# Moving the loads of the last merged-head tiles and the first MLP product at the seam between attention and the MLP of an encoder layer

## The chip, the core and the metric

The kernel runs on one core of one Trainium2 chip. The metric is the device time in microseconds. Shares of the span and times of single instructions come from one execution taken with the hardware profiler.

## What is computed

One encoder layer over 2048 tokens of width 1024: a mixer (eight stick-breaking heads, eight heads of banded softmax attention) and a squared-ReLU MLP, each behind an RMSNorm with shift, scale and gate from a conditioning vector. All in float32.

```python
h = rmsnorm(x, g_norm1[l]) * (1.0 + sc1) + sh1
proj = h @ w_in[l]
...
mixed = jnp.concatenate([o_sb.reshape(B, S, D_SB), o_ca.reshape(B, S, D_CA)], axis=-1)
x = x + gt1 * (mixed @ w_o[l])
h = rmsnorm(x, g_norm2[l]) * (1.0 + sc2) + sh2
x = x + gt2 * (jnp.square(jax.nn.relu(h @ w1[l])) @ w2[l])
```

## The kernel before

Tokens are worked on in four blocks of 512 (TB), the width in eight tiles of 128 (KT = 8); everything is kept transposed, 128 rows of width by 512 tokens. Each float32 operand is split into a high part (a cast on ScalarE, ACT) and a low part (a subtraction on VectorE, DVE), and a product of two is three matmuls on TensorE (PE): a projection of one output tile is 8 tiles x 3 = 24 matmuls of 512 columns. The compiler keeps the order in which the program emits instructions on each engine; DMA loads and stores are issued by SyncE (SP), in that order too.

The attention stage writes the merged heads of token block g, split, into scr_m[g, k] in DRAM (line 803), k = 0 to 7; the stores of the last block (0) are issued by GpSimd (POOL), the very last of them, k = 7, by ACT. Then the output projection of block 1, begun as filler work between the attention's own, is finished, eight rows n (matmuls po, weights ow, residual rows txr from the input), and that of block 0 follows as the steps of class Mixed (line 1974): matmuls pso, which read the eight merged tiles opm_k and weights ow or wo. Mixed.fetch (line 1984) asks for opm_k from scr_m[0, k]. Mixed runs eight steps, n = 5, 6, 7, 0 to 4, with residual rows cxr; a row's result goes to DRAM as scr_x[g, n].

Beside these products the MLP's left side is made for token blocks 3 and 2: right_blocks(1, k) (line 1503) for four values of k. For each k, load asks for four tiles of the normed residual (named ty for k = 0, cy for the rest, from scr_x); DVE multiplies them with the norm row, ACT shifts them, and casts on ACT and subtractions on DVE make seven operands h_1 to h_7 of them, as a fast matrix product of the Strassen and Winograd kind needs. some(k, n) calls piece n of block k: some(0, 0) is the load of ty, some(0, 1) its scaling.

The MLP's steps follow in one list with Mixed's: steps[0] to steps[7] are Mixed, steps[8] (KT) on are class First (line 1587), each one of the seven half-size products in the order OUTER = (1, 5, 6, 3, 7, 2, 4). First.prepare splits a weight tile (opr for the first two, opw for the rest), First.run (line 1630) emits 12 matmuls. Products 1 and 2 share a bank ps, 5 and 3 a second, 6, 7 and 4 a third, ps_s, which starts as a copy of product 1:

```python
if i == 1:
    d["ps", 6] = bank(f"{nm}_s", seeded)
    act.copy(d["ps", 6], ps)
if i in (5, 6):
    d["p", i] = kept(f"p{nm}")
    act.copy(d["p", i], ps)
```

So ACT copies bank 1 to ps_s before product 6, and the banks of products 5 and 6 out to cp before products 3 and 7 add to them.

The order around the change is written out by hand in lines 2104 to 2116: row() emits the rest of one po row (with at most two finished rows' stores held back), and the fetches and pieces stand between the rows. Then the loop of line 2130 runs the steps: for each it prepares coming operands as far as eight buffers reach, runs the jobs listed for the step, and emits its matmuls.

One more thing sets the order at run time. Each DMA that SP or ACT issues adds to one of eight semaphores, named DMAHW0 to DMAHW7, given out in turn as the program is built, and waits until the DMA that had the semaphore last has landed. A waiting issue holds up all that stands behind it on SP.

## Time and profile before

| what | before |
|---|---|
| median of 3 runs | 2511.53 us (2509.88 to 2512.42) |
| span of the profiled execution | 2511.4 us |
| instructions | 39512 |
| PE busy | 2497.0 us (99%) |
| DVE busy | 2027.0 us (81%) |
| ACT busy | 1526.4 us (61%) |
| POOL busy | 787.5 us (31%) |
| DMA | 704.71 MB, mean 281 GB/s |

Of the profiled execution no time is given beside its span; the span stands for it. A row of a timeline gives the start and the length in microseconds from the span's start, the engine (SPq is SP's queue), the source line, the operation, output and inputs by the program's names without their numbers, the shape, and how many alike are merged; in brackets stand the idle time of the engine ahead of the row and what ended it. All operations are recorded by a helper in line 42, so lines tell nothing and names do. PEld is PE's load of weights, which runs beside the matmuls.

### The profile page before, as it was taken

The page shows a single profiled execution, that of the slowest core. Times are in us where ns is not written, and L with a number is a line of the kernel's source. Part 1 is how long each engine was busy: PE and PEld are TensorE (multiplying, and loading weights), DVE is VectorE, ACT ScalarE, POOL GpSimd, SP SyncE. Part 2 cuts the span into 40 slices and gives each one's busy share as a digit, 9 for nine tenths or more (in the row PEclk, how much of TensorE's full clock was granted, in tenths as well). Part 3 has the DMA queues.
Part 4 walks back from the last instruction along what each step waited for, and adds up shares of the span by engine and source line. Part 5 has one row for each costly group of instructions (what it writes and reads, how often), then busy time and mean ns, then how long its engine had stood idle before and what let it go on. Part 6 is the DMA issues. An engine that isn't in the chain of part 4 may idle for free.

```text
span 2511.4 us, 39512 instructions
## 1 busy us (share of the span) xinstructions
PE 2497.0 (99%) x12364; PEld 2093.5 (83%) x12364; DVE 2027.0 (81%) x3571; ACT 1526.4 (61%) x2928; POOL 787.5 (31%) x1174
## 2 busy tenths in 40 slices
PE   9999999999999999999999999999999999999999
PEld 7888888888888888888888888888888888888887
DVE  7656776897789888999868777779877759799998
ACT  6334434778876687666855555567555546577765
POOL 4330144777776677776710000000000000010100
PEclk9999999999999999999999999999999999999999
DMA  9879978789888788866786878996998996888982
GB/s 368 316 301 360 357 274 289 231 263 309 268 263 264 233 252 264 274 193 216 215 321 251 298 284 309 324 354 197 325 326 271 313 364 261 320 250 280 307 277 83
DMA packets 295970, 704.71 MB, mean 281 GB/s; under 512 B 32080, under 2 KB 88400, under 8 KB 284112
## 3 DMA queue, kind: packets, MB, share of 16 engines
q1 hardware_dynamic: 287552, 684.35, 78.8%
q0 software_dynamic: 6768, 13.11, 2.9%
q10 hardware_dynamic: 1440, 4.72, 0.5%
q8 instruction: 98, 1.61, 0.3%
q14 instruction: 112, 0.92, 0.1%
HBM read 473.99 MB, written 228.07 MB: 280 GB/s over the span
## 4 chain that ended last, share of the span: by engine, by line
PE 88%; DVE 4%; DMA 4%; ACT 2%; issue 1%; SPq 0%; POOL 0%; DVEq 0%; ACTq 0%; POOLq 0%
PE ps L42 23%; PE ps_s L42 15%; PE pt L42 11%; PE acc L42 8%; PE wt L42 7%; PE pf L42 6%; PE z L42 5%; PE po L42 4%; PE pq L42 3%; PE cz L42 2%; PE pso L42 1%; PE ct L42 1%; DMA opm<-scr_m 1%; DMA hw<-in_w_dram 1%; PE px L42 1%
## 5 line engine op out<-in xcount | busy, mean ns | idle before, releaser
L42 ACT CAST wth<-wt 128x512 fp32r<-128x512 f32 (+3 forms) x544 | 257.5, 484 | 173.7 <-PE wt L42 160.9
L42 PE MATMUL ps<-h,opw 128*128 128x512 f32 x1512 | 358.6, 389 | 0.0
L42 POOL TENSOR_TENSOR b<-p 128x512 f32<-128x512 f32 (+1 forms) x320 | 292.0, 913 | 154.1 <-DVE p L42 95.6
L42 DVE TENSOR_TENSOR wtl<-wt,wth 128x512 fp32r<-128x512 f32 (+3 forms) x544 | 291.4, 547 | 60.3 <-ACT wth L42 55.8
L42 PEld LDWEIGHTS ps<-h,opw 128*128 128x128 f32 x1512 | 283.6, 188 | 58.9
L42 PE MATMUL pt<-w,ht 128*128 128x512 f32 x1248 | 288.0, 391 | 0.0
L42 PE MATMUL ps_s<-h,opw 128*128 128x512 f32 x1152 | 277.6, 390 | 1.0 <-DVE cp L42 0.6
L42 PEld LDWEIGHTS pt<-w,ht 128*128 128x128 f32 x1248 | 232.9, 188 | 47.6
L42 DVE TENSOR_TENSOR_SCAN p<-z,p,zero 128x512 f32<-128x512 f32 x192 | 245.3, 1279 | 18.6 <-ACT z L42 14.5
L42 PEld LDWEIGHTS ps_s<-h,opw 128*128 128x128 f32 x1152 | 215.7, 188 | 47.4 <-DVE cp L42 1.5
L42 ACT CAST opr<-r 128x512 fp32r<-128x512 f32 x280 | 174.3, 623 | 118.1 <-PE ps L42 66.4
L42 PE MATMUL acc<-wth,v 128*128 128x512 f32 (+3 forms) x544 | 221.3, 410 | 0.0
L42 PE MATMUL ps<-opr,ol 128*128 128x512 f32 x960 | 220.3, 389 | 0.0
L42 PEld LDWEIGHTS ps<-opr,ol 128*128 128x128 f32 x960 | 180.1, 188 | 37.8 <-DVE opr L42 0.4
L42 ACT ACTIVATE z<-z 128x512 f32<-128x512 f32 (+1 forms) x320 | 166.7, 521 | 52.7 <-PE z L42 48.2
L42 DVE TENSOR_TENSOR opr<-r,opr 128x512 fp32r<-128x512 f32 x280 | 185.5, 683 | 13.7 <-ACT opr L42 12.5
L42 PE MATMUL acc<-wtl,v 128*128 128x512 f32 (+3 forms) x544 | 185.6, 347 | 0.0
L42 PE MATMUL z<-k,q 128*128 128x512 f32 (+3 forms) x640 | 182.8, 367 | 0.6 <-DVE p L42 0.6
L42 POOL DMA_DIRECT2D scr_x<-txu x12 | 10.4, 866 | 546.0 <-ACT txu L42 544.1
L42 PE MATMUL ps<-oph,opv 128*128 128x512 f32 x768 | 175.4, 390 | 0.3 <-DVE txo L42 0.2
L42 PE MATMUL wt<-ident,b 128*128 128x128 f32 x1088 | 170.7, 272 | 0.4 <-DVE p L42 0.4
L42 PEld LDWEIGHTS ps<-oph,opv 128*128 128x128 f32 x768 | 144.0, 188 | 31.3 <-DVE txo L42 0.6
(238 smaller groups left out, 5059.9 us busy)
## 6 DMA issues: line engine op xcount, KB each, us to landing
r<-scr_hid SPq DMA_DIRECT2D x80, 512.0 KB, 7.2
q<-scr_q SPq DMA_DIRECT2D x128, 256.0 KB, 5.1
w<-in_w_dram SPq DMA_DIRECT2D x64, 512.0 KB, 5.7
k<-scr_k SPq DMA_DIRECT2D x240, 128.0 KB, 4.6
v<-scr_v SPq DMA_DIRECT2D x120, 256.0 KB, 4.6
wa<-in_w_ada_dram SPq DMA_DIRECT2D x48, 512.0 KB, 6.3
ow<-scr_wo SPq DMA_DIRECT2D x24, 1024.0 KB, 6.6
l<-scr_t SPq DMA_DIRECT2D x20, 1024.0 KB, 7.9
```

The costliest lines, as they stand in the source:

```text
L42: return lambda *x, **y: self.tc.keep_in_program_order(f(*x, **y))
```

## The change

Two edits. In the hand-written order the four later opm tiles move forward: opm_4 and opm_5 are asked for after the first row instead of after the second row and the load of ty, and opm_6 and opm_7 after the second row, ahead of ty, instead of after the third. In the loop, steps[KT], the first MLP product, emits its matmuls and the copy to ps_s ahead of the preparing and the jobs of its turn instead of behind them.

```diff
         steps[0].fetch(0, KT // 2)
         row()
-        row()
-        some(0, 0)
         steps[0].fetch(KT // 2, KT - 2)
         row()
+        steps[0].fetch(KT - 2, KT)
+        some(0, 0)
+        row()
         some(0, 1)
-        steps[0].fetch(KT - 2, KT)
         row()
         some(0, 2)
         some(1, 0)
...
         for n, s in enumerate(steps):
+            if n == KT:
+                s.run()
             while nxt is not None and ready - used + nxt.tiles <= 8 and nxt.ready():
                 nxt.prepare()
...
-            s.run()
+            if n != KT:
+                s.run()
             used += s.frees
```

The instructions stay the same; PE and DVE keep their order. On SP the DMA issues after the load of ow_6 stood so before (each row a DMA, with the semaphores that it waits for; the first number behind a name is its row or tile k, the two after ty its place, the last a running number):

```order
L42 DMA txr_5_16974<-in_xs_dram 128x512 [waits DMAHW6_49,Pool_49]
L42 DMA ow_7_17002<-scr_wo_237 128x2048 [waits DMAHW7_49,PE_49]
L42 DMA txr_6_17004<-in_xs_dram 128x512 [waits DMAHW0_49]
L42 DMA ty_0_11_17008<-scr_x_0_216 128x512 [waits DMAHW1_49]
L42 DMA ty_0_12_17010<-scr_x_0_208 128x512 [waits DMAHW2_49]
L42 DMA ty_0_21_17012<-scr_x_4_220 128x512 [waits DMAHW3_49]
L42 DMA ty_0_22_17014<-scr_x_4_212 128x512 [waits DMAHW4_49]
L42 DMA opm_4_17016<-scr_m_4_164 128x1024 [waits DMAHW5_49,DMASW0_49]
L42 DMA opm_5_17018<-scr_m_5_165 128x1024 [waits DMAHW6_49,DMASW1_49]
```

And so they stand in the changed kernel:

```order
L42 DMA txr_5_16974<-in_xs_dram 128x512 [waits DMAHW6_49,Pool_49]
L42 DMA opm_4_16978<-scr_m_4_164 128x1024 [waits DMAHW7_49,DMASW0_49]
L42 DMA opm_5_16980<-scr_m_5_165 128x1024 [waits DMAHW0_49,DMASW1_49]
L42 DMA ow_7_17006<-scr_wo_237 128x2048 [waits DMAHW1_49,PE_49]
L42 DMA txr_6_17008<-in_xs_dram 128x512 [waits DMAHW2_49]
L42 DMA opm_6_17012<-scr_m_6_166 128x1024 [waits DMAHW3_49,DMASW2_49]
L42 DMA opm_7_17014<-scr_m_7_167 128x1024 [waits DMAHW4_49]
L42 DMA ty_0_11_17016<-scr_x_0_216 128x512 [waits DMAHW5_49]
L42 DMA ty_0_12_17018<-scr_x_0_208 128x512 [waits DMAHW6_49]
L42 DMA ty_0_21_17020<-scr_x_4_220 128x512 [waits DMAHW7_49]
L42 DMA ty_0_22_17022<-scr_x_4_212 128x512 [waits DMAHW0_49]
```

opm_4 and opm_5 now stand ahead of ow_7, opm_6 and opm_7 ahead of ty, and the wait for DMAHW0, whose last user is ACT's store to scr_m[0, 7], has passed from txr_6 to opm_5. On ACT, at the first product of the MLP, the order before was this (opw_0_6 is the weight operand of product 6 for the first pair of weight rows, ps_0_1 its bank 1, ts a sum of weights, w a weight tile):

```order
L42 CAST opr<-ts_0_1_5_17492 128x512
L42 CAST opw_0_6_17528<-ts_0_1_6_17496 128x512
L42 CAST opw_0_3_17531<-ts_0_1_3_17498 128x512
L42 CAST opw_0_7_17534<-w_1_0_17445 128x512
L42 CAST opw_0_2_17537<-w_1_0_17445 128x512
L42 CAST opw_0_4_17540<-w_1_0_17445 128x512
L42 COPY ps_0_1_s<-ps_0_1_17543 128x512
```

And it is now:

```order
L42 CAST opr<-ts_0_1_5_17492 128x512
L42 COPY ps_0_1_s<-ps_0_1_17528 128x512
L42 CAST opw_0_6_17543<-ts_0_1_6_17496 128x512
L42 CAST opw_0_3_17546<-ts_0_1_3_17498 128x512
L42 CAST opw_0_7_17549<-w_1_0_17445 128x512
L42 CAST opw_0_2_17552<-w_1_0_17445 128x512
L42 CAST opw_0_4_17555<-w_1_0_17445 128x512
```

The copy to ps_s has moved ahead of five casts of weights; nothing else on ACT has.

## The prediction

> **What bounds the kernel now.** The page comes first: its span, and the share of the engine that runs the products.

> ```profile
> span 2511.4 us, 39512 instructions
> PE 2497.0 (99%) x12364; PEld 2093.5 (83%) x12364; DVE 2027.0 (81%) x3571; ACT 1526.4 (61%) x2928; POOL 787.5 (31%) x1174
> ```

> TensorE (PE) is busy for 2497.0 of 2511.4 us, so only something that makes PE stand still, or lets it stop standing still, can move the time, and all its gaps together are 14.4 us. The span lies 0.1 us under the median of the three runs shown (2511.53; 2509.88 to 2512.42), so what the sum below adds to the span I add to the median. About 0.2%, 5.0 us, is what a measurement of this kernel can tell from no change. The change touches one place, the seam between the attention stage and the MLP, so the next view is PE's timeline there; a bracket holds the idle time ahead of a row and what ended it.

> ```profile
> 1267.34 22.00 PE L42 MATMUL po<-fx,ow 128*128 128x512 f32 x96
> 1289.18 4.26 PE L42 MATMUL pso<-opm,ow 128*128 128x512 f32 x18
> 1295.02 0.96 PE L42 MATMUL pso<-opm,ow 128*128 128x512 f32 x3 [1.57 <-DMA opm<-scr_m]
> 1296.27 11.86 PE L42 MATMUL pso<-opm,ow 128*128 128x512 f32 x51 [0.29 <-DMA opm<-scr_m]
> 1307.96 27.36 PE L42 MATMUL pso<-opm,wo 128*128 128x512 f32 x120
> 1335.16 5.60 PE L42 MATMUL ps<-h,opr 128*128 128x512 f32 x24
> 1341.17 3.06 PE L42 MATMUL ps_s<-h,opw 128*128 128x512 f32 x12 [0.41 <-ACT ps_s L42]
> ...
> 1344.23 2.72 PE ps L42 x12
> 1346.95 2.98 PE ps_s L42 x12
> ```

> The reader should see four things. A product of 24 matmuls takes 5.44 us: 27.36 us for 120 matmuls is 0.227 to 0.228 each. The 96 matmuls from 1267.34 are rows 4 to 7 of the old projection; the last of them, the one that needs ow_7, begins 72 matmuls in, at 1267.34 + 72 x 0.2275 = 1283.7. In the first row of the merged projection PE waits twice for an opm: 21 matmuls from 1289.18 should end at 1293.97 and the 22nd begins at 1296.27, so 2.3 us are lost. At 1341.17 PE waits 0.41 us for ps_s, and that group takes 3.06 instead of 2.72 us (the last two rows are from the chain of waits: start, length, what), so about 0.75 us are lost; the group at 1346.95 takes 0.26 us more than 2.72. These 3.3 us are all that the change can win here.

> What feeds the seam is the SP queue, in order: each row below is a set of DMA issues. The last two rows are the waits of SP's own queue (total, times, longest) and the chain.

> ```profile
> 1259.45 1.80 SPq L42 DMA_DIRECT2D opm<-scr_m  x4
> 1266.54 0.32 SPq L42 DMA_DIRECT2D ow<-scr_wo  x1
> 1266.96 0.38 SPq L42 DMA_DIRECT2D txr<-in_xs_dram  x1
> 1273.05 0.32 SPq L42 DMA_DIRECT2D ow<-scr_wo  x1
> 1282.28 0.33 SPq L42 DMA_DIRECT2D txr<-in_xs_dram  x1
> 1282.67 1.85 SPq L42 DMA_DIRECT2D ty<-scr_x  x4
> 1284.61 0.85 SPq L42 DMA_DIRECT2D opm<-scr_m  x2
> 1287.06 1.22 SPq L42 DMA_DIRECT2D opm<-scr_m  x2
> ...
> SPq L42 <- DMA scr_m<-os: 8.9, 1, 8.9
> ...
> 1274.59 7.68 DMA scr_m<-os
> ```

> SP issues ow_7 at 1273.05 and then nothing until 1282.28: for 8.9 us its next instruction, the load of txr_6, waits for the store of the last head pair (scr_m<-os), issued by ACT at 1274.59, which takes 7.68 us to land. That load reads nothing of the store. It waits because DMAs take eight semaphores in turn, and the one that falls to it (DMAHW0) was last given to that store. I call this the gate: whichever DMA of SP meets that semaphore stands behind the store, and all of SP behind it.

> Last, the consumers of ty, VectorE (DVE) with ScalarE (ACT), which make the MLP's operands block by block:

> ```profile
> 1286.26 0.69 DVE L42 TENSOR_TENSOR ty<-ty,r 128x512 f32<-128x512 f32 x1 [6.95 <-DMA ty<-scr_x]
> 1287.45 2.18 DVE L42 TENSOR_TENSOR ty<-ty,r 128x512 f32<-128x512 f32 x3 [0.49 <-DMA ty<-scr_x]
> 1334.19 0.68 DVE L42 TENSOR_TENSOR opr<-w,opr 128x512 fp32r<-128x512 f32 x1
> ...
> 1286.26:1298.48 12.22, 10.36 (x45) 7.85 (x44) 10.77 (x18) 7.15 (x11) 0.00 (x0) 1.00 1.02 375
> 1298.48:1310.20 11.72, 11.72 (x53) 9.72 (x52) 10.53 (x18) 6.98 (x11) 0.00 (x0) 1.00 1.04 402
> 1310.20:1321.87 11.67, 11.67 (x53) 9.65 (x52) 10.54 (x19) 6.97 (x11) 0.00 (x0) 1.00 1.04 414
> 1321.87:1333.53 11.66, 11.66 (x53) 9.67 (x52) 10.53 (x18) 7.50 (x12) 0.00 (x0) 1.00 0.77 275
> ```

> DVE waited 6.95 us for the first ty and starts at 1286.26; its fourth ty multiply ends at 1287.45 + 2.18 = 1289.63. From there four blocks follow, 12.2, 11.7, 11.7 and 11.7 us (the columns after the length are the busy times of PE, PEld, DVE, ACT): DVE works 10.5 us of each 11.7 and spends the rest handing tiles to and fro with ACT. Two rows of PE take only 10.9 us, so this chain, and not PE, sets when the first MLP operand is there: 1334.19 + 0.68 = 1334.9, against PE's arrival at 1335.16. PE's stall of 2.3 us hides nearly all that DVE is behind.

> **Part 1, the order of SP's issues.** Nothing is added or taken away; four opm, ow_7, txr_6 and four ty change places. As the rows of the program in the section on the change show, the second opm to be asked for (opm_5) now carries the wait for DMAHW0, and ow_7, txr_6, opm_6, opm_7 and the four ty all stand behind it. Before, ow_7 was ahead of the gate. So the step sooner is worth one tile: opm_4 goes out right behind txr_5, near 1267.4, and the rest of the list leaves when the gate opens.

> When does it open? The store is issued at 1274.59 as before, since ACT, DVE and POOL ahead of it are untouched. How long it takes to land without ow_7 in flight beside it (1 MB less; opm_4, 0.5 MB, in its place) the trace doesn't show. The bounds come from the landing times of all such stores (least, median, most), one load that finds the queues quiet (KB, us to landing) and a stretch in which DMA never rests (its last two columns are the DMA share and GB/s):

> ```profile
> DMA to landing us min/median/max: 2.6/3.7/8.9
> ...
> w<-in_w_dram SPq DMA_DIRECT2D x1, 512.0 KB, 3.7
> ...
> 1287.00:1314.00 27.00, 25.14 (x110) 20.10 (x109) 23.76 (x38) 17.20 (x27) 0.00 (x0) 1.00 1.03 396
> ```

> Over the kernel the stores of an os take 2.6 to 8.9 us, 3.7 in the median, and this one took 7.68. I take 3.7 and add 0.6 for the last 256 KB or so of opm_4 that may be ahead of it at the rate of the third row, 396 GB/s: 4.3, so the gate opens at 1278.9, with 1277.2 and 1282.3 as the ends. [...]

> Behind the gate the first 512 KB (opm_5) should land after 3.7 us, as the second row does, a 512 KB load that finds the queues quiet; what follows lands at 396 GB/s. ow_7 (1.05 MB, 2.65 us): 1278.95 + 3.7 + 2.65 = 1285.3. Up to the fourth ty it is ow_7 1024 KB, txr_6 256, opm_6 and opm_7 1024, ty 1024, together 3.41 MB or 8.6 us: 1278.95 + 3.7 + 8.6 = 1291.25. Multiplied by 0.69 us later, 1291.94, where before it was 1289.63: **the DVE chain starts its first block 2.3 us later** (0.6 at the early end, 5.7 at the late one). The loads of cy, cxr and wo come after; the bytes are the same in both orders, DMA is full here anyway (the row above), and their readers on DVE come 2.3 us later too, so I cost them at nothing. If that cover failed, a cy late by 1 us would add that 1 us to the chain.

> On PE, ow_7 lands at 1285.3 against 1283.7, a new wait of 1.6 us (0 and 5.0 at the ends), and the old wait of 2.3 us is gone, since opm_7 lands near 1288.6 and PE comes to it after 1294. PE reaches the first MLP product 0.7 us sooner, at 1334.5. The operand is there at 1334.9 + 2.3 = 1337.2. So the first product begins 2.0 us later than at 1335.16: what was won on PE is lost in front of DVE.

> **Part 2, the first product emitted ahead of the later casts.** The rows are of ACT, DVE and SP, in that order.

> ```profile
> 1340.55 0.57 ACT L42 COPY ps_s<-ps 128x512 f32<-128x512 f32 x1
> 1345.73 0.63 ACT L42 CAST opw<-ts 128x512 fp32r<-128x512 f32 x1 [1.50 <-DVE ts L42]
> 1346.26 0.58 ACT L42 COPY cp<-ps_s 128x512 f32<-128x512 f32 x1
> ...
> 1338.70 0.75 DVE L42 SCALAR_TENSOR_TENSOR cxr<-pso,mod,cxr 128x512 f32<-128x512 f32 x1
> 1345.01 0.69 DVE L42 TENSOR_TENSOR ts<-w 128x512 f32<-128x512 f32 x1 [2.56 <-DMA w<-in_w_dram]
> ...
> 1329.86 9.93 SPq L42 DMA_DIRECT2D scr_x<-cxr  x3
> 1339.88 0.88 SPq L42 DMA_DIRECT2D w<-in_w_dram  x2
> ```

> On ACT the copy of ps_s comes ahead of five casts of opw; nothing else moves, since PE's and DVE's order is the same. The copy now runs when the first product ends, instead of after five casts, which should take the 0.75 us away at 1341.17. The casts wait behind it, but DVE takes up the first of them only after the cxr row (1338.70), so this costs nothing; were that cover gone, it would be the copy's 0.57 us. What is late next is the group at 1346.95: it writes the bank that ACT must first copy out to cp.

> The copy to cp at 1346.26 stands behind the cast at 1345.73, which waits for DVE's ts (1345.01), which waits 2.56 us for w, which SP issues at 1339.88, right behind the last of three stores of cxr, which waits for DVE's cxr row at 1338.70, part of the same chain. Nothing of this moves forward, so the 0.75 us won at one group is waited out two groups later. I cost part 2 at nothing: 0.75 us gained at most if cp comes sooner.

> **The sum.** At the group of 1346.95 PE is held to the DVE chain: +2.3 us, and after it the order is as before and PE is the bound, so the shift stays. 2511.4 + 2.3 = 2513.7 for the span, 2513.8 beside the median: 0.09%, within what can be told from no change.

> **The rivals.** *All of it is won:* the chain from ty makes up what it loses, and PE alone sets the pace. Then the 2.3 and 0.75 us go and about 2508.5 comes out, 0.12% less. [...] For it: PE's waits at 1295.02 and 1296.27 are real, and opm_4 does leave 17 us sooner. Against it: three blocks in a row of 11.7 us with DVE at 10.5, which leave nothing to catch up with, and three of the four opm stay behind the gate. *Slower:* the store lands as late as it did, 7.68 us after its issue, because what held it was not ow_7. Then the gate opens at 1282.3, PE waits 5.0 us for ow_7 and DVE starts 5.7 us later: 2517.2, +0.23%. It decides from a store of 7.0 us on, where the chain's shift passes 5.0 us. For it: this store took 7.68 us, and 8.9 us have occurred; against it: 0.5 MB less is in the queues. *Nothing to be seen:* the gate opens at 1277.2 and the shift is some tenths, 2511.5 to 2512.

> **How the numbers follow.** The forecast (2513.8) has 0.60, all won 0.12, slower 0.15, nothing 0.13. Faster by over 0.2% would need 5.0 us where at most 3.3 are idle: 0.02 for what I don't see. Slower by over 0.2% is that rival's 0.15, a shade less since its price is close to the bound: 0.14. The remainder, 0.84, is within 0.2%. The range runs from 2510.5, the nothing case less 1 us of the runs' own spread, to the slow rival's 2517.2 and a little; it leaves out the all-won case.

> **What would show it.** In the changed kernel's profile: SP issues one opm near 1267.4 and is then idle until the store lands; ow_7 is issued behind that, at 1279 rather than 1273.05; PE has a wait ahead of the last po row of 0 to 5 us, and none for opm; the first ty multiply on DVE begins near 1289 to 1290, not 1286.26; PE waits ahead of the first ps for DVE's opr; the wait for ps_s at the second group is gone and a longer one for cp stands two groups later. I am wrong if ow_7 still leaves near 1273, if DVE's blocks shrink below 11.7 us, or if the group that stood at 1346.95 comes earlier than it did.

## The result, and the profile after

The changed kernel takes 2514.87 us in the median (2513.35 to 2516.27), the kernel before 2511.73 us in the same series (2509.26 to 2514.12). The ratio is 1.0013, with a 95% interval of 1.0007 to 1.0019: slower by 3.1 us, 1.8 to 4.8. The profiled execution has a span of 2513.6 us, 2.2 us over that of before, and PE's busy time is nearly the same, so the loss is again time in which PE stands still, or runs slowly.

```profile
span 2513.6 us, 39511 instructions
PE 2497.8 (99%) x12364; PEld 2095.1 (83%) x12364; DVE 2028.4 (81%) x3571; ACT 1527.2 (61%) x2928; POOL 788.5 (31%) x1174
```

PE's timeline at the seam, in the changed kernel:

```profile
1266.38 16.56 PE L42 MATMUL po<-fx,ow 128*128 128x512 f32 x72
1283.90 5.72 PE L42 MATMUL po<-fx,ow 128*128 128x512 f32 x24 [0.96 <-DMA ow<-scr_wo]
1289.46 16.48 PE L42 MATMUL pso<-opm,ow 128*128 128x512 f32 x72
1305.78 27.36 PE L42 MATMUL pso<-opm,wo 128*128 128x512 f32 x120
1335.47 0.76 PE L42 MATMUL ps<-h,opr 128*128 128x512 f32 x2 [2.33 <-ACT opr L42]
1336.94 8.03 PE L42 MATMUL ps<-h,opr 128*128 128x512 f32 x22 [0.71 <-DVE opr L42]
...
1350.24 2.88 PE L42 MATMUL ps_s<-h,opw 128*128 128x512 f32 x12
```

This execution arrives at the seam 0.96 us ahead of that of before (its first row here is the one that stood at 1267.34). That is chance, as no instruction ahead of it changed place: near the program's start the granted clock was 0.50 for 3.4 us (from 15.09), against 6.8 us (from 14.83) in the execution of before, and the lead is there from then on. Against that start, ow_7 costs PE a new wait of 0.96 us, and the two waits for opm are gone: 72 matmuls of pso run in one piece. Then PE waits 2.33 and 0.71 us at the first MLP product, and the 22 matmuls that follow take 8.03 us instead of about 5. That was not foreseen. The columns of the next view are the busy times of PE, PEld, DVE, ACT and POOL, then the clock that TensorE was granted, the DMA share and GB/s:

```profile
1335.00:1337.00 2.00, 0.82 (x3) 0.36 (x3) 2.00 (x4) 0.42 (x1) 0.00 (x0) 0.76 0.00 0
1337.00:1339.00 2.00, 2.00 (x5) 1.61 (x6) 1.31 (x3) 0.62 (x1) 0.00 (x0) 0.50 0.34 131
...
1341.00:1343.00 2.00, 2.00 (x7) 1.57 (x6) 0.71 (x2) 1.39 (x3) 0.00 (x0) 0.53 0.39 136
1343.00:1345.00 2.00, 2.00 (x10) 1.68 (x9) 2.00 (x4) 1.79 (x4) 0.00 (x0) 1.00 0.93 306
```

From just after 1336 to nearly 1343 the granted clock was half. SP's queue:

```profile
1266.48 11.48 SPq L42 DMA_DIRECT2D opm<-scr_m  x2
1278.06 0.38 SPq L42 DMA_DIRECT2D ow<-scr_wo  x1
...
1279.01 0.95 SPq L42 DMA_DIRECT2D opm<-scr_m  x2
1280.01 2.10 SPq L42 DMA_DIRECT2D ty<-scr_x  x4
```

What that queue waited for (total, times, longest), and from the view of DMA issues the store that it waited for (KB, us from issue to landing):

```profile
SPq L42 <- DMA scr_m<-os: 10.7, 1, 10.7
```

```profile
scr_m<-os ACTq DMA_DIRECT2D x1, 512.0 KB, 3.9
```

One opm leaves at 1266.48, the second of that row only when the store has landed, after SP has waited 10.7 us for it; ow_7, which left at 1273.05 before, leaves at 1278.06, and the four ty behind it. The store took 3.9 us. On DVE:

```profile
1288.29 0.69 DVE L42 TENSOR_TENSOR ty<-ty,r 128x512 f32<-128x512 f32 x1 [9.93 <-DMA ty<-scr_x]
1289.47 2.12 DVE L42 TENSOR_TENSOR ty<-ty,r 128x512 f32<-128x512 f32 x3 [0.49 <-DMA ty<-scr_x]
...
1336.20 0.68 DVE L42 TENSOR_TENSOR opr<-w,opr 128x512 fp32r<-128x512 f32 x1
```

DVE waits 9.93 us for the first ty instead of 6.95 and ends the fourth multiply at 1289.47 + 2.12 = 1291.59. The row at 1336.20 is the subtraction for the low half of opr, 1334.19 before. Of the seam, 1266 to 1352, the chain of work that ended last is the last view. It can be followed back to 1301.19 and no further; from there DVE and ACT lie on it up to the first product, and PE behind that (shares of the whole seam):

```profile
by line: PE ps L42 12.5%; DVE cy L42 12.4%; DVE h L42 9.1%; ACT cy L42 6.0%; issue 5.9%; PE ps_s L42 5.3%; DVE cxr L42 3.9%; ACT h L42 3.4%; DVE opr L42 0.7%; DVEq L42 0.0%
```

### The profile page after: what moved, and what is told of

It reads as the page before. It is cut to its first block, busy times and chain, and to the rows that moved or that the text cites. A ratio compares the mean times of both kernels' runs of the same rounds, so it can differ in the third digit from the quotient of the medians.

```text
span 2513.6 us, 39511 instructions
## 1 busy us (share of the span) xinstructions
PE 2497.8 (99%) x12364; PEld 2095.1 (83%) x12364; DVE 2028.4 (81%) x3571; ACT 1527.2 (61%) x2928; POOL 788.5 (31%) x1174
## 5 line engine op out<-in xcount | busy, mean ns | idle before, releaser
L42 ACT CAST wth<-wt 128x512 fp32r<-128x512 f32 (+3 forms) x544 | 257.8, 484 | 173.4 <-PE wt L42 160.6
L42 PE MATMUL ps<-h,opw 128*128 128x512 f32 x1512 | 358.6, 389 | 0.0
L42 POOL TENSOR_TENSOR b<-p 128x512 f32<-128x512 f32 (+1 forms) x320 | 292.6, 914 | 153.2 <-DVE p L42 95.7
L42 DVE TENSOR_TENSOR wtl<-wt,wth 128x512 fp32r<-128x512 f32 (+3 forms) x544 | 291.3, 547 | 60.4 <-ACT wth L42 56.0
L42 PEld LDWEIGHTS ps<-h,opw 128*128 128x128 f32 x1512 | 283.6, 188 | 58.9
L42 PE MATMUL pt<-w,ht 128*128 128x512 f32 x1248 | 288.0, 391 | 0.0
L42 PE MATMUL ps_s<-h,opw 128*128 128x512 f32 x1152 | 277.1, 389 | 0.6 <-DVE cp L42 0.6
L42 PEld LDWEIGHTS pt<-w,ht 128*128 128x128 f32 x1248 | 232.9, 188 | 47.6
L42 DVE TENSOR_TENSOR_SCAN p<-z,p,zero 128x512 f32<-128x512 f32 x192 | 245.2, 1278 | 18.7 <-ACT z L42 14.8
L42 PEld LDWEIGHTS ps_s<-h,opw 128*128 128x128 f32 x1152 | 216.0, 188 | 45.8 <-DVE cp L42 1.0
L42 ACT CAST opr<-r 128x512 fp32r<-128x512 f32 x280 | 174.3, 623 | 118.1 <-PE ps L42 66.3
L42 PE MATMUL acc<-wth,v 128*128 128x512 f32 (+3 forms) x544 | 221.2, 410 | 0.0
L42 PE MATMUL ps<-opr,ol 128*128 128x512 f32 x960 | 220.3, 389 | 0.0
L42 PEld LDWEIGHTS ps<-opr,ol 128*128 128x128 f32 x960 | 180.1, 188 | 37.8 <-DVE opr L42 0.4
L42 ACT ACTIVATE z<-z 128x512 f32<-128x512 f32 (+1 forms) x320 | 166.6, 521 | 52.7 <-PE z L42 49.4
L42 DVE TENSOR_TENSOR opr<-r,opr 128x512 fp32r<-128x512 f32 x280 | 185.4, 683 | 13.8 <-ACT opr L42 12.5
L42 PE MATMUL acc<-wtl,v 128*128 128x512 f32 (+3 forms) x544 | 185.5, 347 | 0.0
L42 PE MATMUL z<-k,q 128*128 128x512 f32 (+3 forms) x640 | 182.7, 367 | 0.6 <-DVE p L42 0.6
L42 POOL DMA_DIRECT2D scr_x<-txu x12 | 10.4, 868 | 544.5 <-ACT txu L42 542.7
L42 PE MATMUL ps<-oph,opv 128*128 128x512 f32 x768 | 174.9, 389 | 0.2 <-DVE txo L42 0.2
L42 PE MATMUL wt<-ident,b 128*128 128x128 f32 x1088 | 170.7, 272 | 0.4 <-DVE p L42 0.4
L42 PEld LDWEIGHTS ps<-oph,opv 128*128 128x128 f32 x768 | 144.1, 188 | 30.5 <-DVE txo L42 0.6
## 6 DMA issues: line engine op xcount, KB each, us to landing
r<-scr_hid SPq DMA_DIRECT2D x80, 512.0 KB, 7.5
w<-in_w_dram SPq DMA_DIRECT2D x64, 512.0 KB, 5.7
wa<-in_w_ada_dram SPq DMA_DIRECT2D x48, 512.0 KB, 6.3
```

The lines of the kernel that those rows point to most:

```text
L42: return lambda *x, **y: self.tc.keep_in_program_order(f(*x, **y))
```

## The experiments

**What was to be told apart.** My theory: the chain from ty over DVE sets when PE gets through the first products, the gate (SP's wait for DMAHW0, held by the last store) sets when ty is asked for, and part 2 is worth nothing. The rivals: the early product is to blame or to thank; DMA is simply full, and order decides nothing; the half-speed stretch is the loss. All times below are medians beside the kernel before on the same chip (2511.3 us for the first eight runs, 2511.15 for the last two), with the ratio's interval.

**Each part alone.** The order of SP's issues without the early product, against the changed kernel:

```diff
         for n, s in enumerate(steps):
-            if n == KT:
-                s.run()
...
-            if n != KT:
-                s.run()
+            s.run()
```

> The order of SP's issues alone; the first product is emitted behind the later casts again. My theory (the order carries the whole change, the early product is worth nothing): SP's gate, ow_7 and ty as in the changed kernel, the first multiply of ty near 1288.3, the first MLP product 2.3 us behind PE's arrival, the half-speed stretch behind it, and a time of 2514.9, give or take 1.5. Rival one (the early product is what lets the clock fall, because two matmuls run and then PE waits again): no half-speed stretch and about 2512. Rival two (the early product wins its 0.75 us after all): 0.7 us above the changed kernel.

Measured: 2514.35 us, ratio 1.0012 (1.0003 to 1.0021).

```profile
1284.66 5.72 PE L42 MATMUL po<-fx,ow 128*128 128x512 f32 x24 [1.09 <-DMA ow<-scr_wo]
...
1336.33 0.73 PE L42 MATMUL ps<-h,opr 128*128 128x512 f32 x2 [2.43 <-ACT opr L42]
1337.79 6.87 PE L42 MATMUL ps<-h,opr 128*128 128x512 f32 x22 [0.73 <-DVE opr L42]
1344.50 2.88 PE L42 MATMUL ps_s<-h,opw 128*128 128x512 f32 x12
...
1349.94 2.88 PE L42 MATMUL ps_s<-h,opw 128*128 128x512 f32 x12
```

The order alone gives the loss, 3.0 us against the 3.1 of both parts. The 22 matmuls took 6.87 us, so a half-speed stretch comes too, a shorter one: the early product is not its cause, and the first rival falls. The second (0.7 us) is too small for these times; in the rows the group at 1344.50 does not wait for ps_s.

The other part alone, the early product in the kernel before:

```diff
         for n, s in enumerate(steps):
+            if n == KT:
+                s.run()
...
-            s.run()
+            if n != KT:
+                s.run()
```

> The early first product alone, with the old order of SP's issues. My theory: the first product at 1335.2 as before, no wait for ps_s at the second group, 0.5 to 0.75 us of wait for cp two groups later in its place, no half-speed stretch, 2511 to 2512. Rival (the 0.75 us is kept): the two groups behind the second take 2.72 us each and the end is 0.7 us sooner, near 2510.9. Rival (it costs): 2513 and more.

Measured: 2511.48 us, ratio 1.0000 (0.9991 to 1.0008). PE, then ACT:

```profile
1340.78 2.88 PE L42 MATMUL ps_s<-h,opw 128*128 128x512 f32 x12
...
1347.76 3.01 PE L42 MATMUL ps_s<-h,opw 128*128 128x512 f32 x12 [1.38 <-ACT cp L42]
```

```profile
1346.60 0.62 ACT L42 CAST opw<-ts 128x512 fp32r<-128x512 f32 x1 [1.52 <-DVE ts L42]
1347.13 0.58 ACT L42 COPY cp<-ps_s 128x512 f32<-128x512 f32 x1
```

This is the step of the prediction in plain sight: the copy of ps_s is in time, the groups at 1340.78 and, 2.72 us later, 1343.50 follow at once, and the third waits 1.38 us for the copy to cp, which stands behind a cast that waits for DVE's ts, behind a load of w. It is more than the 0.5 to 0.75 us expected because the fourth ty came 1.1 us later in this execution (T in the table further down). Part 2 is worth nothing here by these rows; the times alone would not show 2 us either way.

**The store on another queue.** In the changed kernel, the store that holds the semaphore goes out on GpSimd's queue; where SP's loads wait for GpSimd's stores, the rows of the change name other semaphores, DMASW0 to DMASW2:

```diff
-            q = act if u is units[-1] else pool if u.ca and u.g == 0 else sp
+            q = pool if u is units[-1] else pool if u.ca and u.g == 0 else sp
```

> The changed kernel with the last store of an os issued by GpSimd instead of ACT, so that no load of SP meets its semaphore; only opm_7, which reads it, waits for it. My theory (the gate and the ty behind it do the harm): opm_5 leaves near 1269, ow_7 near 1273, opm_7 at the store's landing near 1277 to 1278, the ty behind it 1.5 to 2 us sooner than in the changed kernel; no wait of PE for ow_7 or opm; DVE's first multiply near 1286.5, so the first product about as late as in the kernel before, with PE 2 to 3 us early and waiting. 2511.5 to 2512.5 if the clock holds through that wait, up to 3 us more if it falls to half again. Rival (DMA is simply full, and the order and the gate decide nothing): the ty land within 0.5 us of the changed kernel, and 2514.9.

Measured: 2512.76 us, ratio 1.0007 (0.9998 to 1.0016). SP, then PE:

```profile
1272.89 0.32 SPq L42 DMA_DIRECT2D ow<-scr_wo  x1
...
1277.08 5.18 SPq L42 DMA_DIRECT2D opm<-scr_m  x2
1282.32 1.85 SPq L42 DMA_DIRECT2D ty<-scr_x  x4
```

```profile
1289.01 16.48 PE L42 MATMUL pso<-opm,ow 128*128 128x512 f32 x72
...
1334.12 0.73 PE L42 MATMUL ps<-h,opr 128*128 128x512 f32 x2 [1.43 <-ACT opr L42]
...
1348.25 3.02 PE L42 MATMUL ps_s<-h,opw 128*128 128x512 f32 x12 [0.55 <-ACT cp L42]
```

ow_7 leaves at 1272.89 and PE has no wait up to the MLP. But opm_7 stands ahead of ty and needs the store's data, and the store took 7.3 us here, not 4. With the loads asked for earlier the DMA engines are full while it goes out: from 1276 to 1278 their share is 1.07, against 0.04 in the changed kernel. GpSimd's queue may have a part in it too; no run separates the two. So ty leaves at 1282.32, as late as in the kernel before, DVE starts at 1286.45, as late as there, and the lead of PE is spent on the wait in front of the first product, on a half-speed stretch (the 22 matmuls took 6.67 us) and on cp. Counted from the last rows of po, ty even left 1.5 us later than in the changed kernel, where 1.5 to 2 us sooner was expected; but DVE could begin 2.6 us sooner, so DMA is not simply full whatever the order. The gate was gone and a true dependence did nearly the same: what counts is what stands ahead of ty in SP's order.

**ty first.** The same with the four ty ahead of the late opm and ow_7:

```diff
+        some(0, 0)
         steps[0].fetch(KT // 2, KT - 2)
         row()
         steps[0].fetch(KT - 2, KT)
-        some(0, 0)
         row()
         some(0, 1)
```

> As the run before, and the four ty of the first block are asked for right behind the first norm row, ahead of opm_4 to opm_7 and ow_7. My theory (the chain from ty over DVE, not PE, sets when the first MLP product can begin): the ty land before DVE is free, DVE's first multiply is near 1278.5 (7 to 8 us sooner), the operand is there before PE, PE comes to its first product without a wait for opm or opr, no half-speed stretch, and the end is 2508 to 2509. Rival (the chain is held elsewhere, by cy, cxr or ACT, and only its first block moves): the first product still waits over 1 us, 2511 or later. Rival (the cp wait two groups behind the first product stays whatever comes first): 2509.5 to 2510.5.

Measured: 2509.62 us, ratio 0.9993 (0.9984 to 1.0001), 3 us under the run before it in the same series, and above the 2508 to 2509 expected.

```profile
1284.71 5.73 PE L42 MATMUL po<-fx,ow 128*128 128x512 f32 x24 [1.21 <-DMA ow<-scr_wo]
...
1333.80 5.60 PE L42 MATMUL ps<-h,opr 128*128 128x512 f32 x24
```

DVE's four multiplies begin at 1278.82, and PE enters the MLP without a wait. The miss is the 1.21 us for ow_7, which left at 1274.55 and took 10.0 us behind six other loads.

**ow_7 ahead of the late opm.** That wait is taken away by the order ty, ow_7, txr_6, then the four opm (the edit is against the run with the store on GpSimd):

```diff
+        some(0, 0)
+        row()
-        steps[0].fetch(KT // 2, KT - 2)
-        row()
-        steps[0].fetch(KT - 2, KT)
-        some(0, 0)
+        steps[0].fetch(KT // 2, KT)
         row()
         some(0, 1)
```

> The last store on GpSimd, the four ty behind the first norm row, and then ow_7 and txr_6 ahead of all four late opm, the early first product kept. My theory: the 1.2 us wait for ow_7 of the run with ty first goes, opm_7 lands by 1289, 4 us before PE needs it, no wait from the last old row to the second MLP step: 2508 to 2508.5, 1.2 us less than that run and 3.3 less than the kernel before, and that is all that the seam holds. Rival (the DMA queues, with over 8 us from issue to landing here, make another of these loads late): a wait of 0.5 us or more at ow_7 or opm remains, 2509.5 or more.

Measured: 2507.68 us, ratio 0.9984 (0.9975 to 0.9993), a little under the 2508 to 2508.5 expected.

```profile
1289.16 16.48 PE L42 MATMUL pso<-opm,ow 128*128 128x512 f32 x72
...
1332.68 5.60 PE L42 MATMUL ps<-h,opr 128*128 128x512 f32 x24
...
1343.56 2.88 PE L42 MATMUL ps_s<-h,opw 128*128 128x512 f32 x12
```

No wait is left; the group that stood at 1346.95 begins 76.24 us after the first row of the seam (1267.32), which is what its 336 matmuls take at full speed.

Whether part 2 pays once the chain is early was asked with the same kernel and the product emitted at its old place:

```diff
-            if n == KT:
-                s.run()
...
-            if n != KT:
-                s.run()
+            s.run()
```

> The run above with the first product emitted behind the later casts, as in the kernel before. Once the DVE chain is early, cp is there in time, and nothing takes back what part 2 wins. My theory: PE waits 0.3 to 0.8 us for ps_s at the second group and the end is that much above the run above, 2508.5 to 2509. Rival (part 2 is worth nothing even then, as the five casts are done before PE ends the first product): no wait there and the same time within 0.3.

Measured: 2507.81 us, ratio 0.9984 (0.9976 to 0.9993), the same. My theory was wrong and the rival right: ACT copies ps_s at 1336.72, before PE asks for it at 1338.12. With an early chain there is nothing for part 2 to win, and with a late one cp takes it back.

**The gate by itself.** Two runs change only the queue of that store. First in the kernel before, whose order of issues stays as it was:

```diff
-            q = act if u is units[-1] else pool if u.ca and u.g == 0 else sp
+            q = pool if u is units[-1] else pool if u.ca and u.g == 0 else sp
```

> The kernel before, with one word changed: the last store of an os goes out on GpSimd's queue, not ACT's, so that SP no longer meets its semaphore at txr_6. Order of SP's issues and of the first product as before. My theory (the gate held the four ty, and the ty set the end): ow_7 leaves at 1273, txr_6 and the four ty right behind it, by 1275.5 instead of 1284.6; DVE ends its fourth multiply near 1284 to 1286 instead of 1289.6; opm_7 lands before 1292, no wait of PE for it; PE walks through the seam with at most the wait for ps_s, and the end is 2508 to 2508.8 without the change that is studied. Rival (the order of the opm matters in itself): PE still waits 1 us or more for an opm, 2509.5 and more.

Measured: 2507.58 us, ratio 0.9986 (0.9977 to 0.9995). SP, PE, and the chain that ended last:

```profile
1272.87 0.32 SPq L42 DMA_DIRECT2D ow<-scr_wo  x1
...
1274.02 2.08 SPq L42 DMA_DIRECT2D ty<-scr_x  x4
```

```profile
1267.15 22.00 PE L42 MATMUL po<-fx,ow 128*128 128x512 f32 x96
1288.99 16.48 PE L42 MATMUL pso<-opm,ow 128*128 128x512 f32 x72
...
1343.39 2.88 PE L42 MATMUL ps_s<-h,opw 128*128 128x512 f32 x12
```

```profile
by line: PE pso L42 50.6%; PE po L42 25.7%; PE ps L42 13.2%; PE ps_s L42 9.5%; PE acc L42 1.3%
```

The time is a little under the 2508 to 2508.8 expected. One word wins all that the change was after: ty leaves at 1274.02 instead of 1282.67, neither opm nor ow_7 is waited for, and only PE is left on the chain. In the order of before, opm_6 and opm_7 come last, so nothing stands behind their wait but stores and the next block's loads.

Second, the fast order with the store back on ACT:

```diff
-            q = pool if u is units[-1] else pool if u.ca and u.g == 0 else sp
+            q = act if u is units[-1] else pool if u.ca and u.g == 0 else sp
```

> The fastest run so far (ty, then ow_7, then the late opm), with the store put back on ACT's queue. The semaphore that it holds now falls to the second ty. My theory (the gate by itself is harmful, wherever it falls): SP stands from 1267.8 until the store lands, 4 to 7.7 us after 1274.6, with three ty, ow_7 and all late opm behind it; PE waits 1 to 5 us for ow_7, DVE's fourth multiply ends at 1283 to 1287, and the time is 2509 to 2512.5, 1 us or more above the same order without the gate. Rival (the early order alone is what helps, the gate costs nothing): 2508.2 or less, no wait for ow_7.

Measured: 2512.60 us, ratio 1.0008 (0.9999 to 1.0016); the intervals of the two do not meet.

```profile
1266.85 11.63 SPq L42 DMA_DIRECT2D ty<-scr_x  x4
1278.58 0.38 SPq L42 DMA_DIRECT2D ow<-scr_wo  x1
```

```profile
1286.21 7.30 PE L42 MATMUL po<-fx,ow 128*128 128x512 f32 x24 [2.85 <-DMA ow<-scr_wo]
...
1347.74 2.88 PE L42 MATMUL ps_s<-h,opw 128*128 128x512 f32 x12
```

The gate does harm in this order too: SP stands among the four ty, the row of which takes 11.63 us, ow_7 leaves at 1278.58, and PE waits 2.85 us for it. The time is just over the range expected; the clock adds to it, as shown further down.

**The half-speed stretch.** In the changed kernel, 8 small matmuls fill the idle time ahead of the first product:

```diff
                 if i in (1, 5):
                     d["ps", i] = bank(nm, fresh)
+                if self.mb and self.j == 0 and i == 1:
+                    for _ in range(8):
+                        pe.matmul(d["ps", i][:, :P], ones, ones, start=True, stop=True)
```

> The changed kernel with 8 small matmuls of ones ahead of the first MLP product, into its own bank before that is started afresh, about 2.2 us of work in the 2.3 us that PE stands idle there; they add work and change no result. My theory (the half-speed stretch is caused by the idle time, and costs 2 to 3 us of which a later wait for cp would have taken a part anyway): the granted clock stays at 1.00, the first product begins as late as in the changed kernel, the first group ends 3 us sooner, a wait for cp of 1 to 1.5 us stands at the group two behind the second, and the end is 1.3 to 2 us under the changed kernel, near 2513.2. Rival (the stretch costs nothing, because the DVE chain sets the end): 2514.9. Rival (the stretch comes whatever PE does): the clock falls as before.

Measured: 2513.63 us, ratio 1.0009 (1.0000 to 1.0018).

```profile
1338.22 5.31 PE L42 MATMUL ps<-h,opr 128*128 128x512 f32 x22 [0.70 <-DVE opr L42]
...
1350.79 3.06 PE L42 MATMUL ps_s<-h,opw 128*128 128x512 f32 x12 [1.82 <-ACT cp L42]
```

The clock holds (22 matmuls in 5.31 us), and the wait for cp that the prediction named is there, 1.82 us, more than the 1 to 1.5 expected. The time lies 1.2 us under that of the changed kernel, but the intervals overlap, so by these medians the stretch's price cannot be told from none.

The same in the run with the store on GpSimd, with 5 small matmuls:

> The run with the last store on GpSimd, with 5 of the small matmuls (1.4 us) ahead of the first product. There the DVE chain stood where it stands in the kernel before, and PE came 2.6 us early, waited, and lost 2.5 us to the half-speed stretch. My theory: no stretch; the first product 1.0 us ahead of the kernel before; the wait for cp at the group two behind the second grows to 1.5 to 2.5 us, so that the end is that of the kernel before, 2511 to 2512. Rival (without the stretch the whole lead of 1.0 us or more is kept): 2510 or less.

Measured: 2512.14 us, ratio 1.0003 (0.9994 to 1.0011). Here my theory failed on the clock: PE still waited 1.03 and 0.74 us behind the small matmuls, and the 22 matmuls took 6.89 us; the last section shows that both waits fell into one step of the clock there. The end is that of the kernel before within the interval, as expected, and the group behind came without a wait for cp.

**All runs on one scale.** F is the start of the last unbroken row of po (1267.34 before), T the end of DVE's fourth multiply of ty, G the start of the group that stood at 1346.95 in the chain of before (1346.89 in its timeline), each from the timelines.

| kernel | T - F | G - F | G - T |
|---|---|---|---|
| before | 22.29 | 79.55 | 57.26 |
| early product alone | 23.41 | 80.78 | 57.37 |
| store on GpSimd, small matmuls | 23.91 | 81.32 | 57.41 |
| order alone | 25.40 | 82.94 | 57.54 |
| changed, store on GpSimd | 23.15 | 81.08 | 57.93 |
| changed, small matmuls | 26.28 | 84.29 | 58.01 |
| **changed** | 25.21 | 83.86 | 58.65 |
| ty first | 14.37 | 77.73 | 63.36 |
| ty, ow_7 first | 14.37 | 76.24 | 61.87 |
| the same, store on ACT | 17.53 | 80.94 | 63.41 |
| before, store on GpSimd | 17.61 | 76.24 | 58.63 |

In the first seven rows G follows T by 57.3 to 58.7 us, while T itself moves by 4 us: there the chain from ty sets the pace, whatever PE waits for on its way. (In three of them, order alone, store on GpSimd with small matmuls, and changed, PE waits for the chain at the first product only, and the half-speed stretch fills the time up to G.) In the last four, where T is over 4 us earlier, G is F + 76.24 and PE's own waits: PE sets the pace. The changed kernel adds 2.92 us to T - F and 1.39 us to G - T.

## Why the prediction was right, and where its size was off

The time forecast, 2513.8, was 1.1 us under the median, and 2514.87 lies in the range; the sign, and that the difference lies under 0.2%, came as forecast. That 5.0 us is the least that can be told from no change was too cautious: with 21 runs of each kernel the loss is 1.8 to 4.8 us.

**The gate and the store.** Right in kind and nearly in size: opm_5 left at 1277.64, which is 1278.60 on the clock of the execution before, against 1278.9; the store took 3.9 us against 4.3. The slow rival's condition, 7.0 us or more, did not come about in the changed kernel, but it did with the store on GpSimd (7.3), where the DMA share was 1.07 while it went out.

**ow_7 and opm.** Right: a wait of 0.96 us against 1.6, and none for opm.

**The chain.** Right in kind, a little small: T moved by 2.92 us against 2.3. The loads behind the gate came later than 3.7 us and 396 GB/s give: the fourth ty was used 0.6 us later than estimated. That this chain, and not PE, sets the pace was the step on which the sum stood, and the table and the run with one word changed in the kernel before show it: take the gate away and the chain is early, and only PE's matmuls count. The rival "all of it is won" failed for the reason given: the blocks did not catch up, from T to the end of DVE's opr row it is 45.2 us before (1289.63 to 1334.87) and 45.3 now (1291.59 to 1336.88); about 2507.6 was there to win, but by another edit.

**The step that failed** is the last one of part 2, that the 0.75 us won at one group "is waited out two groups later" at the copy to cp: in the changed kernel PE does not wait there. The wait is there in the run of part 2 alone (1.38 us) and with the small matmuls (1.82 us); in the changed kernel the half-speed stretch spent the time before the wait could. The 22 matmuls lost about 2.8 us to it (8.03 us against 5.26 to 5.31 in the runs without it), and G - T is 0.6 to 1.4 us longer than in the other six kernels that the chain holds. So the term "+2.3" should have been 2.9 for the chain, plus what the clock adds beyond the wait it replaces, about 1. Nor is it so that "only something that makes PE stand still" can move the time: at half speed PE is busy and loses time. I took the granted clock of 1.00 for given because the kernel before has no dip at its wait of 1.57 us. The split of that last 1 us rests on single executions and stays an estimate.

**From the seam to the end.** "The shift stays" was right only roughly: 4.31 us more in the seam less the 0.96 us of a lucky start is 3.35, and the profiled spans differ by 2.2. The other 1.2 us lie behind the seam, in small waits of PE that the two executions do not share: PE's matmuls run 3.0 us later than before at 1715.72 (time of before), 2.7 at 1716.32, 1.8 at 1751.88, and 2.2 from 1959.17 on. The medians, 3.1 us apart, rest on 21 runs each and not on these two executions. The prediction held the span of before for nearly the median, 0.1 us under it; but in each run that lists both, the time is 1.7 us above the span, so by that the profiled execution of before was about 1.6 us slower than its median of 2511.53. The forecast does not change by it, as only the shift was added to the median.

## What to carry to other kernels

When a load waits for something that it does not read, look for who last held its completion semaphore: here one late store on another engine's queue stood for 8.9 us in front of nine loads of SP, and putting it on a queue whose semaphores SP's loads do not share won 3.6 us where reordering the loads lost 3.1. Before moving a load forward, ask which of its neighbours feeds the longest chain, and put that one first: the wait that PE showed in front of opm was real, and hidden by a chain of 45 us on DVE that began with another load. And a wait that is taken from PE and given back a little later in one piece may cost more than it was worth, because of the clock: behind waits of 2.33 and 0.71 us 22 matmuls took 8.03 us here, against 5.26 to 5.31.

## What the runs showed of the hardware

**Half speed after short idle times.** The granted clock fell to 0.50 in the changed kernel after waits of 2.33 and 0.71 us with two matmuls between them, with the order alone after 2.43 and 0.73, with the store on GpSimd after 1.43 and 0.73, there with the small matmuls after 1.03 and 0.74, and in the last of the runs on the gate after one wait of 2.85 us. In that last run 24 matmuls took 7.30 us instead of 5.72, and since nothing behind them waited, the 1.6 us were lost for good. It did not fall in the kernel before after 1.57 and 0.29 us, nor with the early product alone after 1.38 us, nor in the changed kernel with the small matmuls after 1.72 us, 0.94 and 0.70, and 1.82.

The length of one wait does not tell these cases apart: the clock fell where the longest wait was 1.03 us, and held after 1.72 and 1.82. In the changed kernel's execution it stood at 0.50 for 3.41 us from 15.09, then at 1.00 for 1317.55 and at 0.50 for 6.83 from 1336.05; in that of before at 0.50 for 6.83 us from 14.83 and then at 1.00 for 2488.31. These are 1, 386 and 2, and 2 and 729 steps of 3.413 us. Cut into such steps, counted in each execution from its first stretch at half clock, the first two rows are from the last of the runs on the gate, the last two from the changed kernel with the small matmuls, at its wait of 1.72 us; the number behind the length is PE's busy time, the third from the end the clock:

```profile
1283.44:1286.86 3.42, 0.65 (x3) 0.60 (x4) 0.69 (x1) 2.36 (x4) 0.00 (x0) 1.00 0.94 347
1286.86:1290.27 3.41, 3.41 (x10) 2.63 (x9) 2.87 (x5) 0.28 (x1) 0.00 (x0) 0.50 1.02 412
...
1282.27:1285.68 3.41, 1.69 (x8) 1.13 (x7) 0.00 (x0) 0.00 (x0) 0.00 (x0) 1.00 0.94 320
1285.68:1289.09 3.41, 3.41 (x17) 2.79 (x16) 0.00 (x0) 0.00 (x0) 0.00 (x0) 1.00 1.00 390
```

**The same store took 3.1 to 8.1 us.** On ACT's queue the 512 KB store took 7.68 us in the kernel before and 7.8 with the early product alone, with ow_7 asked for 1.5 us ahead of it; where SP had issued nothing for 7 us it took 3.9 in the changed kernel, 4.3 with the order alone, 4.9 with the small matmuls and 3.1 in the last run on the gate. On GpSimd's queue, where SP's loads went on, it took 7.3 to 8.1; what that queue itself adds is open, as no run has the store there without the loads. In the kernel before with the store on GpSimd it took 7.9 us, about as long as the 7.68 on ACT's queue, and PE waited for nothing in the seam: late as it was, it did no harm there.
